# LayerNorm and GELU on one core: loading gamma and beta behind the first four rows of x, on SyncE's queue instead of ScalarE's

## The chip, the cores and the metric

The kernel runs on one core of a Trainium2 chip. The metric is the device time of one execution in microseconds, and lower is better. Each kernel was run several times beside the kernel before on the same chip; times are medians. The span of a profile is about 2 us shorter than the clocked time (318.5 against 320.3 us for the kernel before).

## The reference

```
x: 8 x 1024 x 2048 float32; gamma, beta: 2048 float32
mean = np.mean(x, axis=-1, keepdims=True)
var = np.var(x, axis=-1, keepdims=True)
normalized = (x - mean) / np.sqrt(var + eps)
out = gamma * normalized + beta
return 0.5 * out * (1 + np.tanh(np.sqrt(2 / np.pi) * (out + 0.044715 * out ** 3)))
```

The input is 67.1 MB and the output the same. Gamma and beta are 8 KB each.

## The kernel before

The 8192 rows are taken as 16 buffers of 128 partitions x 4 rows x 2048 columns, 4.19 MB each. There are five slots in SBUF, and the result of a buffer overwrites its input, so the load of buffer b + 5 has to wait until buffer b has been stored. SyncE issues the loads. Buffer 0 is loaded row by row, so that work can start early, and so is buffer 3 (SPLIT):

```
for b in range(B):
    s = slot(b)
    if stored(b):
        sy.wait_ge(s_store[s], stored(b))
    for q in range(R):
        if b == 0:
            sy.dma_start(out=xts[s][:, q:q + 1], in_=xg[0, :, q:q + 1]).then_inc(s_first[q], 16)
        elif b == SPLIT:
            sy.dma_start(out=xts[s][:, q:q + 1], in_=xg[b, :, q:q + 1]).then_inc(s_load[s], 16)
    if b not in (0, SPLIT):
        sy.dma_start(out=xts[s], in_=xg[b]).then_inc(s_load[s], 16 * R)
```

Per row VectorE takes the statistics, GpSimd the scale and the bias, ScalarE normalizes into yk, VectorE multiplies by gamma, TensorE adds beta in PSUM, and ScalarE applies GELU and stores. ScalarE also loads gamma and beta at its start, and makes the copy g_t of gamma over all partitions. Nothing can be multiplied by gamma before that copy is there:

```
ac.preload_act_table(ACT.Gelu_apprx_tanh)
for k, (p, src) in enumerate(((64, gamma), (0, beta), (32, beta))):
    ac.dma_start(out=row(p), in_=src.rearrange("(o k f) -> o k f", o=1, k=K)).then_inc(s_par[k], 16)
ac.wait_ge(s_m, 1)
...                                    # two conversions of beta
ac.activation(out=g_t, in_=pss[0], func=ACT.Identity)._wait_ge(s_tg, 1).then_inc(s_c, 1)
for t in range(T + 1):
    ...                                # yk of row t, then GELU of row t - 1
    if by_row(b):                      # the last buffer: one store a row
        ac.dma_start(out=og[b, :, q:q + 1], in_=xt[:, q:q + 1])...
    elif q == R - 1:                   # one store a buffer
        ac.dma_start(out=og[b], in_=xt)...
```

TensorE broadcasts gamma from one partition to 128 by a product with ones (eight float32 matmuls), which waits for gamma's load (s_par[0]). VectorE waits for the copy g_t before the statistics of row 1.

## Time and profile before

| | kernel before |
|---|---|
| time, median (lowest to highest) | 320.3 us (320.06 to 320.59) |
| bytes moved | 134.2 MB, 421 GB/s over the span |
| busiest compute engine | ScalarE, 79% of the span |
| DMA share from 2.7 to 314.3 us | 1.00, at 430 GB/s |
| TensorE's wait for gamma ends | 6.06 us |
| first store issued | 36.02 us |
| last store issued | 310.32 us |

The DMA share is the mean busy share of the 16 DMA engines. The windows view counts the whole time of a packet in the window in which it starts, so in a window of a few microseconds the share is rough, and can pass 1. The packet records of the trace have the start, the duration and the size of each packet, which is what one DMA engine moves at a time: a load of a whole buffer is 128 packets of 32 KB, a load of one of its four rows 128 of 8 KB.

The chain of waits follows the end of the program back, at each step to what released it. A transfer in it carries its time in the queue as well as its own time.

### The profile page before, as it was taken

How to read it: one execution, taken by the hardware profiler on the slowest of the kernel's cores; microseconds unless marked ns; L12 is line 12 of the kernel's file. 1: busy time of each engine (PE TensorE's matmuls, PEld its weight loads, DVE VectorE, ACT ScalarE, POOL GpSimd, SP SyncE). 2: the span in 40 equal slices, each digit the busy share in tenths (PEclk: the TensorE clock that was granted, in tenths of full speed). 3: DMA queues.
4: the chain of work that ended last, by engine and by line, in shares of the span. 5: the costliest groups of instructions: out<-in, count | busy, mean ns of one | idle time of the engine just before them, and what ended most of it. 6: DMA issues, size and time to landing. Idle time of an engine off the chain costs nothing.

```text
span 318.5 us, 2090 instructions
## 1 busy us (share of the span) xinstructions
PE 244.3 (77%) x520; PEld 57.2 (18%) x520; DVE 247.5 (78%) x386; ACT 251.7 (79%) x132; POOL 110.6 (35%) x201
## 2 busy tenths in 40 slices
PE   2769999999999989687795868958589595886860
PEld 1212222222212112111121112212112121111110
DVE  3499999999999897786968968599686986869810
ACT  2769999999999989698696967969589695995970
POOL 1144444444444444232443333333332433324300
DMA  7999999999999999999999999999999999999995
GB/s 289 438 457 401 394 434 430 444 424 436 432 424 444 417 453 416 440 440 416 457 403 457 420 436 444 411 461 403 453 432 424 449 407 457 424 432 403 453 396 209
DMA packets 6002, 134.26 MB, mean 421 GB/s; under 512 B 704, under 2 KB 752, under 8 KB 752
## 3 DMA queue, kind: packets, MB, share of 16 engines
q1 hardware_dynamic: 3168, 67.11, 49.4%
q10 hardware_dynamic: 2832, 67.13, 49.0%
q14 instruction: 2, 0.02, 0.0%
HBM read 67.13 MB, written 67.11 MB: 421 GB/s over the span
## 4 chain that ended last, share of the span: by engine, by line
DMA 64%; ACT 14%; DVE 10%; POOL 5%; PE 3%; issue 1%; ACTq 0%; DVEq 0%; POOLq 0%; SPq 0%
DMA xt<-in_x_dram 32%; DMA out_dram<-xt 30%; ACT yk L195 9%; DVE sts L149 7%; ACT xt L202 4%; POOL ves L135 3%; DVE zg L158 2%; PE ps L220 2%; DMA rows<-in_gamma_dram 2%; POOL rss L137 2%; POOL nms L139 1%; DVE mvs L155 1%; PE ps L237 1%; ACT g_t L191 1%; ACTq L205 0%
## 5 line engine op out<-in xcount | busy, mean ns | idle before, releaser
L149 DVE BATCH_NORM_STATS2 sts<-xt 128x6 f32<-128x512 f32 x256 | 157.7, 679 | 33.5 <-DMA xt<-in_x_dram 31.9
L195 ACT ACTIVATE yk<-xt,nms,rss 128x2048 bf16<-128x2048 f32 x64 | 133.7, 2090 | 48.9 <-POOL nms L139 42.9
L237 PE MATMUL ps<-zg,ident 128*128 128x512 bf16 x256 | 120.8, 627 | 55.8 <-DVE zg L158 54.7
L233 PE MATMUL ps<-b_hl,ones_b 33*128 33x512 bf16 x256 | 120.6, 624 | 2.2 <-PEq L228 2.2
L202 ACT ACTIVATE xt<-ps 128x2048 f32<-128x2048 f32 x64 | 118.9, 1858 | 1.5 <-PE ps L237 1.5
L135 POOL TENSOR_SCALAR ves<-mvs 128x1 f32<-128x1 f32 x64 | 38.5, 602 | 179.2 <-DVE mvs L155 179.2
L158 DVE TENSOR_TENSOR zg<-yk,g_t 128x2048 bf16<-128x2048 bf16 x64 | 76.5, 1195 | 19.2 <-ACT yk L195 19.2
L237 PEld LDWEIGHTS ps<-zg,ident 128*128 128x128 bf16 x256 | 27.6, 130 | 149.0 <-DVE zg L158 113.7
L233 PEld LDWEIGHTS ps<-b_hl,ones_b 33*128 33x128 bf16 x256 | 27.0, 127 | 92.1 <-issue 88.4
L139 POOL TENSOR_SCALAR nms<-mvs,rss 128x1 f32<-128x1 f32 x64 | 35.7, 558 | 6.3
L137 POOL TENSOR_TENSOR rss<-ves,mhalf 128x1 f32<-128x1 f32 x64 | 35.3, 552 | 5.3
L155 DVE BATCH_NORM_AGGREGATE mvs<-sts 128x2 f32<-128x24 f32 x64 | 16.9, 264 | 2.2
L220 PE MATMUL ps<-rows,ones 1*128 1x512 f32 x8 | 7.2, 1076 | 6.1 <-DMA rows<-in_gamma_dram 6.1
L188 ACT ACTIVATE b_hl<-rows 1x2048 bf16<-1x2048 f32 x1 | 1.9, 1909 | 5.3 <-DMA rows<-in_beta_dram 5.3
L166 DVE TENSOR_TENSOR b_hl<-rows,b_hl 1x2048 bf16<-1x2048 f32 x1 | 2.3, 2280 | 2.8 <-ACT b_hl L189 2.8
L220 PEld LDWEIGHTS ps<-rows,ones 1*128 1x128 f32 x8 | 2.5, 327 | 9.2 <-DMA rows<-in_gamma_dram 6.1
L191 ACT ACTIVATE g_t<-ps 128x2048 bf16<-128x2048 f32 x1 | 1.9, 1877 | 1.9 <-PE ps L220 1.9
L184 ACT ACT_TABLE_LOAD x1 | 1.3, 1283 | 0.9 <-SPq L107 0.9
L189 ACT ACTIVATE b_hl<-rows 1x2048 bf16<-1x2048 f32 x1 | 1.9, 1908 | 0.0
L161 DVE MEMSET b_hl<- 33x1024 uint32 x1 | 0.9, 912 | 1.2 <-SPq L107 1.2
L126 POOL MEMSET ones<- 65x128 f32 x1 | 0.2, 202 | 0.5 <-SPq L107 0.5
L130 POOL TENSOR_SCALAR_AFFINE_SELECT ident<-ident 128x128 bf16<-128x128 bf16 x1 | 0.3, 295 | 0.1
(7 smaller groups left out, 0.9 us busy)
## 6 DMA issues: line engine op xcount, KB each, us to landing
out_dram<-xt ACTq DMA_DIRECT2D x15, 4096.0 KB, 32.6
xt<-in_x_dram SPq DMA_DIRECT2D x14, 4096.0 KB
xt<-in_x_dram SPq DMA_DIRECT2D x8, 1024.0 KB, 8.4
out_dram<-xt ACTq DMA_DIRECT2D x4, 1024.0 KB, 8.6
rows<-in_beta_dram ACTq DMA_DIRECT2D x2, 8.0 KB, 5.9
rows<-in_gamma_dram ACTq DMA_DIRECT2D x1, 8.0 KB, 5.1
```

The costliest lines, as they stand in the source:

```text
L135: po.tensor_scalar(out=ves[:, c], in0=mvs[:, k, 1:2], scalar1=float(eps), scalar2=1.0, op0=ALU.add, op1=ALU.mult)._wait_ge(s_a, k + 1).the ...
L137: po.tensor_tensor(out=rss[:, c], in0=ves[:, c], in1=mhalf, op=ALU.pow)._wait_ge(s_q, 2 * k + 1).then_inc(s_q, 1)
L139: po.tensor_scalar(out=nms[:, c], in0=mvs[:, k, 0:1], scalar1=rss[:, c], scalar2=-1.0, op0=ALU.mult, op1=ALU.mult)._wait_ge(s_q, 2 * k + 2 ...
L149: ins = ve.bn_stats(out=sts[:, q, j, :], in_=xr[:, j, :])
L155: ve.bn_aggr(out=mvs[:, q], in_=sts[:, q])._wait_ge(s_o, count).then_inc(s_a, 1)
L158: ve.tensor_tensor(out=zgs[q % 2], in0=yks[q % 2], in1=g_t, op=ALU.mult)._wait_ge(s_n, count).then_inc(s_z, 1)
L191: ac.activation(out=g_t, in_=pss[0], func=ACT.Identity)._wait_ge(s_tg, 1).then_inc(s_c, 1)
L195: ac.activation(out=yks[t % 2], in_=xts[slot(b)][:, q], func=ACT.Identity, scale=rss[:, q:q + 1], bias=nms[:, q:q + 1])._wait_ge(s_p, t + ...
L202: ins = ac.activation(out=xt[:, q], in_=pss[i % 2], func=ACT.Gelu_apprx_tanh)._wait_ge(s_t, i + 1)
L220: ins = pe.matmul(pss[0][:, cols(j)], lhsT=ones[64:65], rhs=rows[64:65, j * K // nsub:(j + 1) * K // nsub, :d // K], start=True, stop=True)
L233: ins = pe.matmul(ps[:, cols(j)], lhsT=ones_b, rhs=b_hl[:, cols(j)], start=True, stop=False)
L237: ins = pe.matmul(ps[:, cols(j)], lhsT=ident, rhs=zgs[k % 2][:, cols(j)], start=False, stop=True)
```

## The change

It takes the three small loads off ScalarE's queue, which then carries nothing until the first store. They go to SyncE's queue behind the four rows of buffer 0, so that x comes first and gamma follows when row 0 to 3 are in.

```
                         elif b == SPLIT:
                             sy.dma_start(out=xts[s][:, q:q + 1], in_=xg[b, :, q:q + 1]).then_inc(s_load[s], 16)
+                    if b == 0:
+                        for k, (p, src) in enumerate(((64, gamma), (0, beta), (32, beta))):
+                            sy.dma_start(out=row(p),
+                                         in_=src.rearrange("(o k f) -> o k f", o=1, k=K)).then_inc(s_par[k], 16)
                     if b not in (0, SPLIT):
...
                 ac.preload_act_table(ACT.Gelu_apprx_tanh)
-                for k, (p, src) in enumerate(((64, gamma), (0, beta), (32, beta))):
-                    ac.dma_start(out=row(p), in_=src.rearrange("(o k f) -> o k f", o=1, k=K)).then_inc(s_par[k], 16)
                 ac.wait_ge(s_m, 1)
```

## The prediction

> **What bounds the kernel now.** I read the page first: its span, its row of DMA slices and its HBM line.
>
> ```profile
> span 318.5 us, 2090 instructions
> DMA  7999999999999999999999999999999999999995
> HBM read 67.13 MB, written 67.11 MB: 421 GB/s over the span
> ```
>
> Each digit is one fortieth of the span, 8 us. The DMA engines are nine tenths busy or more in all slices but the first and the last, while no compute engine passes 79% of the span. To find where the saturation starts and ends I asked for the windows view, which prints a stretch of time, the busy time of PE, PEld, DVE, ACT and POOL, the clock, the DMA share and GB/s:
>
> ```profile
> 0.00:2.70 2.70, 0.00 (x0) 0.00 (x0) 0.91 (x1) 1.28 (x1) 1.00 (x9) 1.00 0.30 58
> 2.70:314.30 311.60, 244.30 (x520) 57.16 (x520) 246.58 (x385) 250.43 (x131) 109.56 (x192) 1.00 1.00 430
> 314.30:318.50 4.20, 0.00 (x0) 0.00 (x0) 0.00 (x0) 0.00 (x0) 0.00 (x0) 1.00 0.06 25
> ```
>
> From 2.7 to 314.3 us the DMA share is 1.00 at 430 GB/s: 311.6 us x 430 GB/s = 134.0 MB, all but 0.2 MB of what the kernel moves. So the time is 2.7 us of start, 134.2 MB at 430 GB/s, 4.2 us for the last write to land, and 1.8 us between span and clocked time (320.3 - 318.5). A change that doesn't alter the bytes can gain almost nothing, and can lose only by making the DMA engines run dry.
>
> The chain of waits tells another story, and is the trap here. In order of time it begins (start, duration, what):
>
> ```profile
> 0.92 5.09 DMA rows<-in_gamma_dram
> ...
> 6.06 7.21 PE ps L220 x8
> ...
> 13.29 1.89 ACT g_t L191
> ...
> 66.99 1.77 ACT xt L202
> ...
> 68.79 26.55 DMA out_dram<-xt
> 95.33 0.02 issue
> 95.35 33.54 DMA xt<-in_x_dram
> ```
>
> Gamma's load is the first real link; PE broadcasts it (7.2 us), ScalarE copies it (1.9 us), and from there an unbroken compute chain runs to the issue of the third store at 68.8 us. Only then do transfers carry the chain. But its transfers of 26.6 and 33.5 us each move 4.19 MB, which alone take 4.19 / 0.430 = 9.75 us: most of each is queueing behind the other stream. A link that is queueing can shrink when what precedes it is late, so the chain's length doesn't add up like the DMA's.
>
> **What the Trainium skill says.** (1) "DMA: Bandwidth & Descriptors", section "Issuing engines are not separate DMA queues": DMAs issued from different engines run on the same 16 DMA engines and interleave; spreading them saves only the sequencer's issue time. So moving three loads between queues changes no bandwidth. The trace agrees: loads (q1) and stores (q10) share one 430 GB/s. (2) Same page, "Queues, rings and completion order": each queue is a ring per DMA engine, consumed in ring order, and the engine alternates between rings packet by packet. Behind four rows on one ring, gamma therefore starts after them. The packet records of the trace agree with both halves: in 40 to 52 us the loads of buffer 3 still run in 8 KB packets, the first store in 32 KB packets, and the store gets 3.9 MB while the loads get 1.1 MB. (3) Same page, "Where 436 GB/s comes from": a ceiling of 435 GB/s at the ports. The 430 measured is 99% of it.
>
> **The change, part by part.** *Removed:* three DMA issues of 0.60 us on ScalarE's queue (timeline: 0.92 to 2.80 us). ScalarE next waits for beta until 7.51 us, so this is worth 0. The 48 parameter packets also no longer mix with row 0 and row 1; 24 KB at 430 GB/s is 0.06 us, so 0.
>
> *Added on SyncE:* the same three issues, 1.8 us, before buffer 1's load. That issue slides from 3.12 to about 4.9 us. The ring then still holds most of the 4.19 MB of buffer 0, until 2.7 + 9.75 = 12.5 us. Hidden with 7 us to spare: 0.
>
> *Moved: gamma's landing.* In the packet records the last 8 KB packet of the fourth row ends at 13.41 us. Row 0's last packet ended at 5.51 and VectorE, which waits for it, started at 5.86, so from packet end to wake is 0.35 us. Gamma's 512 B packet per engine (0.03 us) follows: landing at about 13.8 instead of 6.06. Call the shift D = 7.7 us. Beta follows within 0.2 us, and its work (two ScalarE copies of 1.9, one VectorE subtraction of 2.3 us) stays inside PE's 7.2 us plus the 1.9 us copy. So g_t is ready at 15.2 + 7.7 = 22.9 us, and everything behind it moves by D:
>
> ```profile
> 13.29 1.88 ACT L191 ACTIVATE g_t<-ps 128x2048 bf16<-128x2048 f32 x1 [1.93 <-PE ps L220]
> 15.19 2.09 ACT L195 ACTIVATE yk<-xt,nms,rss 128x2048 bf16<-128x2048 f32 x1
> 36.02 0.36 ACTq L210 DMA_DIRECT2D out_dram<-xt  x1
> ```
>
> First store at 36.0 + 7.7 = 43.7 us, second at 52.4 + 7.7 = 60.1, third at 68.8 + 7.7 = 76.5.
>
> *Does the DMA run dry meanwhile?* There are five slots, so five loads need no store: 20.97 MB. Store 0 makes it 25.17 MB. Until these are moved the engines have work as long as store 0 is there before the loads end, at 2.7 + 20.97 / 0.430 = 51.5 us; it comes at 43.7 plus at most 4.0 us (36.02 to its first packet at 40.00 in the kernel before). All six transfers end at 2.7 + 25.17 / 0.430 = 61.2 us, whatever their order. The next work is store 1, issued at 60.1. With the other ring empty a store's first packet came 1.1 us after issue (293.91 to 295.0), so 61.2: the join is just closed, with nothing to spare. Load 5 waits for store 0 (SyncE sees a store about 0.8 us after its last packet: 53.63 and 54.43) and starts at about 63 to 66. Store 1 alone fills the engines till then, as stores alone do at the end (419 GB/s in 310 to 314.3 us).
>
> *After that* compute makes a buffer every 16.4 us (store issues at 36.02, 52.40, 68.79), the DMA moves one in and one out in 8.39 / 0.430 = 19.5 us. So each store is issued some 3 us earlier against the DMA than the one before, the stores' backlog grows, and no further dry spot can occur. The loads have run ahead meanwhile: at 61 us 20.97 MB are in, before about 19.2 MB. Half of that lead is given back while load 5 is late, so I expect the last load some 4 us earlier, near 281 us (chain before: 285.0).
>
> *The end.* After the last load the kernel before needs 25.3 us of compute to the last store's issue (285.0 to 310.3), while the DMA has some 30 us of stores to write: the two were about balanced. With the load at 281 the last issue falls at 306, and the DMA, not compute, ends the kernel where its bytes end.
>
> Sum: 0 + 0 + a dry spot of about 0.5 us (0 by the centre, but the sixteen engines don't finish together) - 0.2 us for a tail with more backlog (the share was 0.97 to 0.98 in 285 to 310 us, 0.6 us of idling, of which a part may go) = +0.3 us. **Predicted: 320.6 us.**
>
> **The rivals.** *The chain carries the delay:* the end moves by D, to 328.0 us, 2.4% slower. For it: gamma heads the chain and compute is unbroken to 68.8 us. Against it: DMA at 1.00 throughout, so the store's 26.6 us must shrink. *The dry spot is real:* a longer landing of gamma, or a store's first packet 3.7 us after issue (52.40 to 56.11, other ring busy), leaves the engines idle for 1 to 3 us near 61 us: 321.5 to 323.5. For it: the join has no slack. Against: the other ring is empty just then. *Faster:* loads run alone for longer and the tail is fed better. At most the 0.6 us idling of the tail can be won: 319.7.
>
> **Range and chances.** The floor is 320.3 less 0.6 and some scatter of the runs (320.06 to 320.59): 319.2. The upper end is a dry spot of 2.5 us: 323.0. 2% is 6.4 us, which neither reaches; only the first rival does, and I give it 4%. Faster by 2% would need fewer bytes: 1%. Within 2%: 95%.
>
> **What would show each step.** Windows: share 1.00 and some 430 GB/s from 2.7 to 314 us again; single microseconds from 58 to 66 us show the dry spot or its absence. Timeline: gamma's wait on PE ends near 13.8, g_t starts near 21, first store issued near 43.7. Waits: SyncE's first wait for a store ends near 62 instead of 54.4. Chain: the last load near 281 us, last store issued near 306. I am wrong if the DMA share falls below 0.9 for several microseconds anywhere after 60 us, or if the end moves by as much as the first store does.

## The result, and the profile after

The changed kernel takes 320.35 us (320.33 to 320.82, four runs) beside 320.26 us for the kernel before. The ratio is 1.0005, with a 95% interval of 0.9988 to 1.0023: no difference. (A ratio is the mean time of one kernel's runs over that of the other's of the same rounds, so not quite the ratio of the medians.) Executions over 1.5% slower than the fastest of the same kernel are left out of the means.

All of the start has moved, and the end has not. The timeline of the changed kernel (start, duration, engine, line, what; in brackets the idle time before it and what ended it):

```profile
13.61 7.19 PE L222 MATMUL ps<-rows,ones 1*128 1x512 f32 x8 [13.61 <-DMA rows<-in_gamma_dram]
...
20.84 1.88 ACT L193 ACTIVATE g_t<-ps 128x2048 bf16<-128x2048 f32 x1 [3.19 <-PE ps L222]
22.75 2.09 ACT L197 ACTIVATE yk<-xt,nms,rss 128x2048 bf16<-128x2048 f32 x1
...
43.58 0.38 ACTq L212 DMA_DIRECT2D out_dram<-xt  x1
```

Gamma is there at 13.61 us instead of 6.06, and the first store is issued at 43.58 instead of 36.02: both 7.6 us later. Now the windows view (stretch, busy times of the five engines, clock, DMA share, GB/s) and the page's span:

```profile
span 318.3 us, 2090 instructions
```

```profile
0.00:2.70 2.70, 0.00 (x0) 0.00 (x0) 0.91 (x1) 1.28 (x1) 1.00 (x9) 1.00 0.29 61
...
2.70:314.30 311.60, 244.39 (x520) 57.35 (x520) 246.06 (x385) 250.00 (x131) 109.65 (x192) 1.00 1.00 430
...
60.00:63.00 3.00, 3.00 (x8) 0.61 (x6) 2.44 (x6) 2.49 (x2) 1.10 (x4) 1.00 0.96 415
```

The second line is that of the kernel before over again: DMA share 1.00 and 430 GB/s over the same 311.6 us. The third is the place where the engines might have run dry. Its 0.96 is no idle time, but comes from counting packets where they start. When each packet of the records is spread over the time that it took, the share is 1.00 in every single microsecond from 3 to 312 us: there was no dry spot.

SyncE's waits for stores (total, number, longest) in the kernel before and after:

```profile
SPq L122 <- DMA out_dram<-xt: 240.3, 11, 47.2
```

```profile
SPq L126 <- DMA out_dram<-xt: 243.7, 11, 54.7
```

The longest is the first one, the wait of load 5 for store 0. It grew by 7.5 us, as the store came later. In the packet records load 4 then ends at 57.2 us and load 5 begins at 67.4, so the load ring was empty for 10 us, where the kernel before had load 5 follow load 4 at once (69.1 and 69.0). The stores filled the engines alone. That is how the delay vanishes: it was not made up by faster work, but taken by the other stream.

The chain of waits of the changed kernel (start, duration, what) shows where its compute chain now ends, and how the last buffer goes:

```profile
2.91 10.66 DMA rows<-in_gamma_dram
...
140.06 1.77 ACT xt L204
...
141.85 36.42 DMA out_dram<-xt
...
178.29 24.21 DMA xt<-in_x_dram
...
255.74 24.21 DMA xt<-in_x_dram
...
303.33 1.88 ACT xt L204
```

The last load in the chain of the kernel before:

```profile
250.80 34.20 DMA xt<-in_x_dram
```

The unbroken compute chain from gamma on now lasts to about 142 us, where it was 68.8 before. Read alone, this chain says that compute has become the bound, which the unchanged time denies. And the last load of the chain has landed by 280.0 us (before: 285.0), 5 us *earlier* in a kernel whose start is 7.6 us later; the last store is issued at 305.24 us (before: 310.32). With the stores starting later, the loads ran ahead.

### The profile page after: what moved, and what is told of

It is laid out like the page before. It is cut to its first block, busy times and chain, and to the rows that moved or that the text cites. A ratio compares the mean times of both kernels' runs of the same rounds, so it can differ in the third digit from the quotient of the medians.

```text
span 318.3 us, 2090 instructions
## 1 busy us (share of the span) xinstructions
PE 244.4 (77%) x520; PEld 57.4 (18%) x520; DVE 247.0 (78%) x386; ACT 251.3 (79%) x132; POOL 110.6 (35%) x201
## 4 chain that ended last, share of the span: by engine, by line
DMA 44%; DVE 19%; ACT 18%; POOL 9%; PE 3%; issue 2%; SPq 1%; ACTq 0%; POOLq 0%; DVEq 0%
DMA out_dram<-xt 25%; DMA xt<-in_x_dram 15%; ACT yk L197 13%; DVE sts L153 12%; DVE zg L162 5%; POOL ves L139 5%; ACT xt L204 4%; DMA rows<-in_gamma_dram 3%; POOL rss L141 3%; PE ps L222 2%; POOL nms L143 1%; DVE mvs L159 1%; PE ps L239 1%; ACT g_t L193 1%; SPq L118 1%
## 5 line engine op out<-in xcount | busy, mean ns | idle before, releaser
L222 PE MATMUL ps<-rows,ones 1*128 1x512 f32 x8 | 7.2, 1076 | 13.6 <-DMA rows<-in_gamma_dram 13.6
L222 PEld LDWEIGHTS ps<-rows,ones 1*128 1x128 f32 x8 | 2.5, 325 | 16.7 <-DMA rows<-in_gamma_dram 13.6
```

What stands on the lines that cost most here:

```text
L222: ins = pe.matmul(pss[0][:, cols(j)], lhsT=ones[64:65], rhs=rows[64:65, j * K // nsub:(j + 1) * K // nsub, :d // K], start=True, stop=True)
```

## The experiments

The theory: the time is the start of the DMA, the bytes at some 430 GB/s, and what the engines stand idle. The rivals: the delay of gamma is carried to the end by the chain; the start is hidden whatever its length; the queue matters and not the time of landing. Ten kernels were run, all with correct results.

| kernel | first store issued | last load's last packet | last store issued | time, us | against before |
|---|---|---|---|---|---|
| before | 36.0 | 283.3 | 310.3 | 320.26 | |
| changed | 43.6 | 278.4 | 305.2 | 320.35 | 1.0005 |
| act_wait | 50.6 | 283.5 | 310.3 | 324.36 | 1.0120 |
| behind_b1 | 53.6 | 285.6 | 312.4 | 327.52 | 1.0227 |
| first | 34.4 | 290.2 | 317.0 | 325.78 | 1.0136 |
| first_hold | 38.1 | 285.6 | 312.6 | 322.64 | 1.0066 |
| first_nosplit | 34.4 | 283.6 | 310.5 | 322.09 | 1.0053 |
| before_nosplit | 35.9 | 278.1 | 305.2 | 319.99 | 0.9986 |
| pool_early | 37.0 | 281.8 | 308.8 | 320.71 | 1.0009 |
| split4 | 43.5 | 280.1 | 307.1 | 320.97 | 1.0014 |
| norow_before | 35.9 | 283.2 | 309.7 | 324.18 | 1.0148 |
| norow_after | 43.8 | 279.7 | 306.2 | 320.50 | 1.0011 |

The third column is from the packet records of the trace, the second and the fourth from the timelines. Times are medians of all runs; the ratios are each to the kernel before in the same rounds.

### More delay: behind_b1

```
-                    if b == 0:
+                    if b == 1:          # and after the load of buffer 1
                         for k, (p, src) in enumerate(((64, gamma), (0, beta), (32, beta))):
```

> Gamma and beta on SyncE's queue behind buffer 1 as well. Gamma lands near 23.6 us, 17.5 later than before; first store issued near 53.5. My theory: the five free loads end at 51.5 us, so the engines run dry until store 0's first packet at 54.6 (3.1 us), again between store 0's end (64.4) and load 5's first packet (66.4; 2.0 us), and once more for about 1.5 us near 86 us before store 2: 6.6 us in all, 326.9 us. Rival, chain carries the delay in full: 320.3 + 17.5 = 337.8. Rival, the start is hidden whatever its length: 320.3.

Measured: 327.52 us (327.33 to 327.86), 7.3 us over the kernel before in the same rounds, which had a median of 320.27. Gamma came at 23.61 us, 17.55 later. Windows of this kernel:

```profile
48.00:52.00 4.00, 3.28 (x9) 0.73 (x8) 3.92 (x7) 4.00 (x4) 1.30 (x2) 1.00 0.88 377
52.00:54.00 2.00, 1.95 (x6) 0.49 (x5) 2.00 (x3) 1.52 (x1) 1.78 (x3) 1.00 0.00 0
54.00:56.00 2.00, 2.00 (x6) 0.49 (x5) 1.67 (x4) 1.89 (x1) 0.26 (x2) 1.00 1.23 524
...
64.00:66.00 2.00, 1.28 (x4) 0.20 (x3) 1.59 (x2) 2.00 (x2) 1.59 (x3) 1.00 0.01 4
...
92.00:94.00 2.00, 1.96 (x5) 0.42 (x4) 1.97 (x4) 2.00 (x2) 1.03 (x1) 1.00 0.81 262
```

The DMA engines stand still around 52 to 54 us (the five free loads are in, store 0 isn't there yet) and 64 to 66 us (store 0 is out, load 5 isn't there yet), as foretold. By the packet records these two gaps are 2.6 and 2.1 us of idle engines, and the third one, expected to be about 1.5 us, is only 0.25. That is 4.9 us of the 7.3; 6.6 were expected. The rest is in longer packets: all packets together keep an engine busy 2.3 us longer than in the kernel before. There 3 packets of 32 KB take over 1.35 us, here 94 do, up to 2.3 us, where 1.2 is usual. They lie mostly in groups of up to 16, near the times at which a transfer starts or one of the two streams stops (15 of them at 66 to 68 us, when load 5 starts). Why they take longer is not shown. So the sum of 326.9 was met (327.52) with a part of it in the wrong place.

By 280 us the packet records of this kernel add up to 116.2 MB, those of the kernel before to 119.5: 3.2 MB at 430 GB/s are 7.5 us. The loss thus comes before the tail. Of 17.55 us of delay, 7.3 reach the end. The chain rival (337.8) and the rival that hides everything (320.3) both fall.

### The delay without the move: act_wait

```
                 ac.preload_act_table(ACT.Gelu_apprx_tanh)
+                ac.wait_ge(s_first[R - 1], 16)      # kernel before, otherwise
```

> Kernel before, but ScalarE waits for the fourth row of buffer 0 before it issues gamma and beta on its own queue: the delay without the move to the other queue. Issue near 13.3, landing 4.2 us later (before: 0.92 issue, 5.12 first packet), near 17.8: a shift of 11.7 us, first store issued near 47.7. My theory: store 0's first packet comes at 51.5, just as the loads end; store 0 ends at 61.3, load 5 starts at 63.3, store 1 at 65.2, so dry for about 2.0 us: 322.3 us. Chain theory: 332.0. If the queue itself mattered rather than the time of landing, this would equal the kernel before, 320.3.

Measured: 324.36 us (323.96 to 324.73). That is 2.1 us more than expected. Gamma was issued at 13.32 us as foreseen, but landed at 20.65, which is 7.3 us later and not 4.5, so that D is 14.6 and not 11.7 us. At that time the other ring was full of 32 KB packets instead of 8 KB ones. The window of the dry spot:

```profile
61.00:62.00 1.00, 1.00 (x3) 0.12 (x1) 0.54 (x1) 1.00 (x2) 0.79 (x3) 1.00 0.55 238
62.00:64.00 2.00, 1.28 (x4) 0.44 (x4) 2.00 (x4) 2.00 (x2) 0.82 (x1) 1.00 0.00 0
64.00:66.00 2.00, 2.00 (x6) 0.42 (x4) 1.97 (x4) 2.00 (x2) 0.54 (x1) 1.00 0.95 295
```

This is the gap between store 0 and load 5 that the changed kernel bridges with store 1: there store 1 was issued at 59.95 us, here at 66.97. By the packet records the engines are idle for 2.3 us in it, close to the 2.0 expected, so the longer delay didn't make it much longer. As in behind_b1 the rest is in longer packets, 1.8 us an engine. By 280 us 117.6 MB are moved, 1.9 MB less than before, or 4.3 us: again the loss comes before the tail. So the same small loads on ScalarE's queue cost 4.1 us if they come late enough. This speaks for the time of gamma's landing as the cause, and not the queue; but no run has gamma land near 13.6 us from ScalarE's queue, which would show it directly. The three delays of 7.6, 14.6 and 17.6 us cost 0.1, 4.1 and 7.3 us: at least 7.6 us are free. The prediction's join at 61 us puts the end of the free part near 8 us; where between 7.6 and 14.6 it lies, no run shows.

### Less delay: first

```
                     for q in range(R):              # changed kernel, with the block "if b == 0"
                         if b == 0:                  # of gamma and beta moved up to ahead of this loop
```

> Gamma and beta on SyncE's queue ahead of row 0. My theory (the time is set by the start, bytes at 430 GB/s and the end): three issues of 0.60 us push row 0's first packet from 2.2 to about 4.0 us, so everything that the DMA engines do is 1.8 us later: 322.1 us. Rival (the chain of waits carries gamma's landing): gamma lands near 2.8 instead of 6.06, the first yk starts about 3 us earlier (row 0's statistics then bound it), so 317.2 us. The two differ in sign.

Measured: 325.78 us in the median of six runs, between 323.71 and 338.18; two of them (331.37 and 338.18) count as slow, and the other four have a mean of 324.9. The sign is that of the theory and not of the chain: gamma was there at 3.01 us, the first store was issued at 34.41 (1.6 us sooner than in the kernel before), and the kernel is slower. But it is 4.5 us slower and not 1.8. Two windows of the profiled run, which had a span of 323.2 us:

```profile
0.00:4.00 4.00, 0.99 (x1) 0.49 (x2) 0.91 (x1) 1.71 (x2) 1.00 (x9) 1.00 0.03 6
297.00:301.00 4.00, 3.28 (x9) 0.76 (x8) 3.44 (x6) 3.56 (x2) 1.61 (x3) 1.00 0.04 16
```

The first is the late start: x's first packet comes at 4.06 us and not at 1.92, a loss of 2.1. The second was not expected: 4 us near the end almost without traffic. The last load ends at 290.2 us. ScalarE applies GELU to a buffer's last row only after the yk of the next buffer's first row, so the store of the buffer before waits for this load too: it is issued at 300.59, and all other stores have drained by 297 but for a few packets. The step missing in my expectation was the tail: I had read it as balanced, but didn't ask what a lead lost by the loads does to it. Two runs test that reading.

### Is the dry tail due to the loads' lost lead? first_hold and first_nosplit

```
+                ac.wait_ge(s_first[R - 1], 16)      # first_hold: kernel "first", g_t held back
                 ac.activation(out=g_t, in_=pss[0], func=ACT.Identity)...
```

> Gamma and beta first on SyncE's queue as in the run before, but ScalarE's copy g_t, and with it all that follows, held until the fourth row of buffer 0 has landed (near 16). Question: that run took 325 us instead of 322.1; its trace has 2.1 us of late start and 4 us without traffic near 297 to 301, after the last load (290.4). Theory: the stores, starting 3.7 us sooner against the loads, held the loads back, so the last buffer's compute came late. With the first store back at about 38.9 us, the dry spot at the end goes and the late start stays: 322.4 us. If the stall has another cause: 325 again.

```
-SPLIT = 3
+SPLIT = -1          # first_nosplit: kernel "first", buffer 3 loaded in one piece
```

> Gamma and beta first, buffer 3 loaded in one piece of 32 KB packets instead of four of 8 KB. Same theory, other handle: the first store now takes half of the engines instead of four fifths, the loads lead, the last load ends at 286 or before, no dry spot at the end: 322.4 us. If the stall has another cause: 325 again.

Measured: 322.64 us (322.38 to 322.99) and 322.09 us (322.00 to 322.20). The same stretch of the tail in first_hold and in first_nosplit:

```profile
297.00:301.00 4.00, 3.36 (x9) 0.77 (x8) 3.53 (x6) 3.56 (x2) 1.52 (x3) 1.00 1.11 475
```

```profile
297.00:301.00 4.00, 3.36 (x8) 0.85 (x8) 3.56 (x6) 3.51 (x3) 1.18 (x4) 1.00 1.12 483
```

The dry spot is gone in both, the late start remains, and with it some 2 us. The two edits have little in common: one makes the first store later, the other gives the first store half of the engines in place of four fifths. Both let the loads lead (last load's last packet at 285.6 and 283.6 instead of 290.2). With that the 4.5 us of "first" are accounted for as about 2 us of start and the rest of tail. Why its single runs scatter from 323.7 to 338.2, with the clock at 1.00 in all, while no other kernel did so by more than 3 us, stays open; a tail with no backlog of stores is a likely place, but no run shows it.

### The lead of the loads as slack: norow_before and norow_after

The changed kernel issues its last store 5 us earlier. If that is slack, an edit that hurts the tail must cost it less than the kernel before.

```
     def by_row(b):
-        return b == B - 1
+        return False        # the last buffer in one store; once on each of the two kernels
```

> Kernel before with the last buffer stored in one piece instead of row by row. Its last issue stays at about 309 us (a little less than 310.3, as three issues on ScalarE are gone), and the engines run dry from 305.5, when the store of buffer 14 ends, to about 310.2: +4.7 us, near 325.0 us. If the tail of the kernel before were not balanced between compute and DMA as I read it, nothing much would change: 320.5.

> Changed kernel with the last buffer stored in one piece. My theory: its loads end 4 to 5 us earlier, so the last issue falls at about 304 us (305.24 less the three issues), before the store of buffer 14 ends (304.7 to 305.7), and the engines run dry for 0 to 1 us: 320.3 to 321.3 us, some 4 us faster than the same edit of the kernel before. Rival, the two kernels are equal because the start of the program has no effect on its end: the same as the edit of the kernel before, near 325.

Measured: 324.18 and 320.50 us; ratios to the kernel before of 1.0148 (interval 1.0105 to 1.0192) and 1.0011 (0.9994 to 1.0027). The tail of the first, and of the second:

```profile
305.00:310.00 5.00, 2.00 (x5) 0.44 (x4) 0.78 (x1) 3.16 (x2) 0.00 (x0) 1.00 0.02 7
```

```profile
305.00:310.00 5.00, 0.00 (x0) 0.00 (x0) 0.00 (x0) 1.13 (x1) 0.00 (x0) 1.00 0.75 321
```

In the edited kernel before, compute still works in this window and the DMA waits for it (share 0.02). In the edited changed kernel compute is all but done and the DMA works on, after about 2 us of idle engines between 304 and 307. So the two kernels are equal in time but not in state: with the same edit one is 4.1 us over the kernel before and the other 0.4, so what the change does is put some 4 us of slack at the end, for which the kernel as it stands has no use.

### Packet sizes: before_nosplit and split4

```
-SPLIT = 3
+SPLIT = -1          # before_nosplit: on the kernel before
+SPLIT = 4           # split4: on the changed kernel, whose first store comes later
```

> Kernel before with buffer 3 loaded in one piece. Theory: first store takes half instead of four fifths of the engines and lands near 59 instead of 53.6, loads lead by some microseconds, last load near 280, the DMA has no less to do: 320.3, within 0.5. Rival: the early landing of the first store was what kept the engines fed: 321.5 or more.

> Changed kernel, but buffer 4 instead of buffer 3 is loaded in four pieces of 8 KB packets, so that the later first store again meets small load packets, as in the kernel before. My theory: store 0 gets about four fifths of the engines and ends near 60 us or earlier, load 4 ends last and load 5 follows it without a gap, but the bytes are the same and the engines were not dry: 320.3 us, within 0.5. Rival: the early store's lead matters, and the changed kernel lost something by it that this wins back: 1 us or more faster.

Measured: 319.99 us (0.9986, interval 0.9965 to 1.0006) and 320.97 us (1.0014, 0.9995 to 1.0033). Neither is a difference clear of noise, and split4 missed its half microsecond by a little. Yet the transfers moved: store 0 of before_nosplit ended at 59.0 us instead of 53.4, its last load at 278.1 instead of 283.3, while store 0 of split4 ended at 60.4, and its load 5 began at 65.3 where the changed kernel's began at 67.4. That load 5 would follow load 4 without a gap was wrong: load 4 ended at 62.9. In these two runs the sizes decide who goes first, and the total stays. Loading buffer 3 in pieces gains the kernel before nothing that these runs show.

### A run that didn't make its case: pool_early

```
-                    ac.dma_start(out=row(p), ...)   # in ScalarE's block
+                    po.dma_start(out=row(p), ...)   # at the top of GpSimd's block
```

> Kernel before with gamma and beta issued from GpSimd instead of ScalarE, so that gamma lands before row 0 (about 3.5 to 4.5 us) without delaying the loads of x. Chain of waits: first yk and all behind it some 2 to 3 us earlier, so 317.5 us. My theory as it now stands: an earlier first store holds the loads back, the last buffer's compute comes later and the tail runs dry for 1 to 3 us: 321 to 323 us. Were the DMA the only thing: 320.3.

Measured: 320.71 us (1.0009). The run didn't make the condition it was for: GpSimd issued gamma at 1.45 us, but it landed at 7.01, after row 0 and 0.95 us later than before, not earlier. A shift of 1 us with no effect agrees with the theory, and tells little. Whether an earlier gamma without a late start would hurt the tail stays open.

No kernel of these beats the kernel before by more than the noise. With a DMA share of 1.00 from 2.7 to 314.3 us in the kernel before and in the changed one, a change of gamma's landing had next to nothing to win there.

## Why the prediction was right

- **The bound.** DMA share 1.00 at 430 GB/s over 311.6 us, before and after. The forecast was 320.6 us, and 320.35 was measured. Shown by the windows, and by behind_b1 and act_wait, which lost time where their engines stood idle, before the tail.
- **The two small terms** (+0.5 for a dry spot, -0.2 for the tail) were not seen. There was no dry spot, and the tail's "0.6 us of idling" was the windows' way of counting: in the packet records the engines of the kernel before are idle for 0.2 us in 285 to 310 us. The forecast was right as "no change"; that it came within 0.3 us tells nothing more.
- **Issues removed and added: 0.** SyncE issued buffer 1's load at 4.80 us instead of 3.12, as worked out, and buffer 1's last packet still ended at 22.7 us (before: 22.9).
- **The shift D.** Forecast 7.7 us from the fourth row's last packet, measured 7.55 (gamma) and 7.56 (first store). Its parts were less exact, and cancelled by luck. On one zero the prediction had the fourth row's last packet at 13.17 us (its 13.41) and TensorE's start 0.6 us after it; measured were 12.64 us and 1.0.
- **The join at 61 us.** Forecast closed "with nothing to spare". In the packet records store 0 ends at 62.6 us, and store 1 has begun at 61.6, so the engines never waited. act_wait and behind_b1 show that it opens when the stores come 7 or 10 us later still. Load 5 was put at 63 to 66 us and began at 67.4, without harm, as the stores filled the engines. (The "0.8 us" after which SyncE sees a store was misread: 54.43 is the end of the next load's issue. The landing is marked at 54.06, 0.7 us after the last packet at 53.39.)
- **The end.** Last load near 281 us, last issue at 306; measured 280.0 and 305.2, so the lead grew by 5 us and not 4. That the DMA ends the kernel there, with compute to spare, is shown by the norow pair.
- **The chain rival** fell in four runs: in the change itself, in "first" with its opposite sign, and in act_wait and behind_b1, which lost 4.1 of 14.6 and 7.3 of 17.6 us.
- **What the prediction left out,** and only "first" brought to light: the tail is balanced, so that stores moved forward against the loads can cost time, as they did there. The prediction asked only what a later gamma does, for which it didn't matter.

## What to carry to other kernels

Where the DMA engines are busy throughout, ask of a delay at the start only whether they run out of queued transfers: add up the bytes that may go without it, and divide by the rate. If they do run out, the loss can be larger than the gap itself (4.1 us for a gap of 2.3 in act_wait). A chain of waits in which transfers take several times their own duration is a chain of queueing, and its compute part can be 8 us later, or 70 us longer, without the time changing. And stores that begin too early against the loads can cost: in "first", where the loads began 2.1 us later and the stores 1.6 us sooner, the last buffer arrived with nothing left to hide its compute. Whether earlier stores alone do this, no run shows.

## What the Trainium skill lacked or had wrong

- "DMA: Bandwidth & Descriptors", section "Queues, rings and completion order", has the engines alternate between rings by packet, but not what follows from unequal packets: in 40 to 52 us of the kernel before, the stream of 32 KB packets moved 3.9 MB beside 1.1 MB of the stream of 8 KB packets.
- The same page, section "Latency and other measured facts", gives about 600 ns to the first byte of a DMA issued from SyncE or ScalarE. It doesn't say from where it counts. Here it took 1.0 us from the start of an issue of 0.4 to 0.8 us with the engines idle (0.93 to 1.92 us; 1.4 us for gamma in "first"), and 3.5 to 4.0 us with the other ring full (52.40 to 55.86, and 0.92 to 4.88). An 8 KB load landed 5.1 us after issue beside 8 KB packets and 7.3 us after it beside 32 KB packets.
- The same page, section "Issuing engines are not separate DMA queues", calls the sequencer's issue time usually small relative to the DMA itself, and doesn't speak of what waits behind it. Ahead of the first load of a DMA-bound kernel three issues of 0.6 us delayed the first packet of x by 2.1 us, and the two kernels without a dry tail beside this (first_nosplit and first_hold) took 322.1 and 322.6 us instead of 320.4.
- No page tells how the order of two streams at the start comes back at the end: the same bytes at the same rate ended in a tail with some 4 us of slack (the changed kernel) or 4 us dry ("first").
- No page tells that 32 KB packets take up to 2.3 us instead of 1.2 near the times at which a stream starts or stops (94 such packets in behind_b1, 57 in the changed kernel, 3 in the kernel before).
